# gate_a's matrix-vector product in a latent-flow layer: slabs taken in two runs of four and eight of one, each loaded one call ahead

## The chip, the cores and the metric

The kernel runs on one core of a Trainium2 chip. The core has a matrix engine (TensorE, PE in the profile, with PEld for its weight loads), a vector engine (VectorE, DVE), a scalar engine (ScalarE, ACT), GpSimd (POOL) and SyncE (SP), whose queue issues most of the loads from DRAM. On-chip memory is SBUF; TensorE writes to PSUM, which has eight banks here. The metric is the device time of one execution in microseconds (us), lower is better.

## The reference, cut to what matters

One layer of a flow-matching backbone with 128 context tokens and 256 latent tokens, width 2048, all in float32. A condition vector of each of the two groups is turned into six modulation vectors of width 2048:

```
mod = silu(cond) @ ada_w + ada_b          # ada_w: 2048 x (6 * 2048)
shift_a, scale_a, gate_a, shift_f, scale_f, gate_f = mod
h   = rmsnorm(x) * (1 + scale_a) + shift_a
q, k, v, o, gates, u = split(h @ w_in)
hm  = rmsnorm(bidirectional mLSTM(q, k, v, gates)) * sigmoid(o)
hp  = pooling mixer(u)
x   = x + gate_a * rmsnorm(concat(hm, hp) @ w_out)
h   = rmsnorm(x) * (1 + scale_f) + shift_f
x   = x + gate_f * rmsnorm(relu(h @ w1)**2 @ w2)
```

The change concerns how the second half of gate_a (columns 1024 to 2047 of it) is computed. It is not needed before the attention's output has gone through w_out.

## The kernel before, in words

All 384 tokens go through together. Activations stand transposed, as 16 k-tiles of 128 channels. Each float32 operand of a large product is split into a high and a low part (ScalarE copies the high part, L134; VectorE subtracts, L135), and three matmuls (`mm3`, L143 to L145) make one product.

The stages are: scale_a and shift_a with the projections u and v (to 203 us of the profile); the q and k gemms of head group 0, with pooling and gates beside them; three more q and k pairs, and then four o gemms, with attention beside them; the output projection `w_out`; then the MLP.

`gemm_T` walks through its weights in steps. One step loads one slab of weights of 512 KB by SP (`load_w`), splits it, and runs 4 k-tiles x 2 halves x 3 = 24 matmuls. A q or k gemm has 4 steps, so a pair has 8. At the end of a step the gemm calls its *feeds*: each feed is a Python generator with a rate, adds the rate to its due time at every step, and runs to its next `yield` once for every whole unit that is due. A feed thus sets between which gemm steps its instructions stand in the program.

The program is then ordered by a scheduler, in these stages for all engines: among instructions that it reckons to be ready, the one that stands first in the program goes first. It also gives out buffers: a load is put in an engine's queue when a buffer of its tag is free. So loads can run far ahead of their users, in the order of the program, and each engine's queue, SP's too, is then worked off in that fixed order.

Two feeds multiply the conditions by pieces of ada_w here, in two ways:

- `ada1` is gate_a's second half, by `ada_mat` (L215) on TensorE. It has 16 slabs of 512 KB: 4 parts of 256 columns by 4 groups of 4 of the 16 k-tiles. Each call loads one slab (L228) and issues its 4 matmuls (L232), each with 32 weight columns at one of four column groups of the array, so that the four run beside one another. A float32 matmul of this kind is recorded twice. The 64 matmuls add up in one PSUM bank. At the end ScalarE copies the bank (L238), four matmuls gather the rows (L241), and `ada_finish` adds the bias and multiplies by the norm's weights on VectorE (L249, L257). Its rate is 0.35.
- `ada2` is `mid_vec`, five times `ada_vec`: scale_f, shift_f and gate_a's first half, each in pieces of 1024 columns, by VectorE. A slab of 512 KB is loaded one ahead (L269), then two VectorE operations per slab (L280, L282) add it to an accumulator, of which there is one. After 16 slabs TensorE sums the accumulator over the partitions (`adav`, L293), and later `adaf` (L299) and `ada_finish` close it. Its rate is 1.5 from the second q and k pair on.

Slabs of both feeds have the tag `ada`, with four buffers (`N_ADA = 4`). Attention (L572 on) is a feed at rate 1 with its own VectorE, ScalarE and GpSimd work; its matmuls are `mb`, `s`, `k`, `sk`, `cu`, `num` and `inter`, and the feeds of a step are called with attention's first, then `ada1`, then `ada2`.

```
ada1 = Feed(ada_mat([(2, 8 + 2 * b, 2) for b in range(4)]), RATE_MAT)
...
qk(0, (fxt, fg_, fp_, ada1))
...
for g in range(1, 4):
    fa.append(Feed(attention(g - 1), 1.0))
    qk(g, (*fa[-2:], ada1, ada2))
```

Of the kernel before, what the change touches and what calls it, by code (L numbers as in the profile page):

```python
# [7 lines left out]
F32 = mybir.dt.float32  # L8
# [5 lines left out]
P = 128  # L14
D = 2048
# [13 lines left out]
N_ADA = 4  # L29
# [7 lines left out]
S_FIRST, S_LAST, N_LAST = 1, 6, 2  # L37
LAG = 4
RATES = (1.5, 1.3, 1.3)
RATE_MAT = 0.35  # L40


@with_exitstack
def hymba_kernel(
# [6 lines left out]
    nc = tc.nc  # L51
# [6 lines left out]
    adap = ada_scope.enter_context(tc.tile_pool(name="adap", bufs=1, side="right"))  # L58
# [6 lines left out]
    def bank(name):  # L65
        return psum.tile([P, 512], F32, tag="ps", name=name)
# [38 lines left out]
    cT = adap.tile([P, 16, 38], F32, name="cT")  # L105
# [106 lines left out]
    mod = const.tile([P, 6, KT, 2], F32, name="mod")  # L212
    aw = ada_w.rearrange("(p j) n -> p j n", j=16)

    def ada_mat(parts, tags=("ada",), raws=None):  # L215


        n, nk = len(parts), parts[0][2]
        w, nj = nk * P, 8 // nk
        ps = bank(f"ada_{parts[0][0]}_{parts[0][1]}")  # L220
        for b, (i, k0, _) in enumerate(parts):
            c0 = i * D + k0 * P
            for j0 in range(0, 16, nj):
                tag = tags[b % len(tags)]
                raw = raws.pop(0) if raws else None
                if raw is None:
                    raw = (wp if tag == "lo" else adap).tile([P, nj, w], F32, tag=tag, name=f"ada_raw_{i}_{k0}_{j0}", bufs=N_W if tag == "lo" else N_ADA)
                    nc.sync.dma_start(raw, aw[:, j0:j0 + nj, c0:c0 + w])  # L228
                for a in range(nj):
                    j = j0 + a  # L230
                    g = j % 4
                    nc.tensor.matmul(ps[32 * g:32 * g + 32, 0:w], cT[:, j, 6 - 2 * b:38 - 2 * b], raw[:, a, :],  # L232
                                     start=b == 0 and j < 4, stop=b == n - 1 and j >= 12)
                if b < n - 1 or j0 + nj < 16:
                    yield
        sb = adap.tile([P, 512], F32, tag="adasb", name=f"ada_sb_{parts[0][0]}_{parts[0][1]}", bufs=1)
        with tc.high_priority():
            nc.scalar.activation(sb[:, 0:w], ps[:, 0:w], AF.Copy)  # L238
        yield
        for k in range(nk):  # L240
            nc.tensor.matmul(ps[:, 256 + 8 * k:256 + 8 * k + 2 * n], sb[:, k * P:(k + 1) * P], cst[:, C_SEL, 0:2 * n], start=True, stop=True)  # L241
        for b, (i, k0, _) in enumerate(parts):
            ada_finish(i, k0, nk, ps[:, 256:256 + 8 * nk].rearrange("p (k r) -> p k r", r=8)[:, :, 2 * b:2 * b + 2])
        yield

    def ada_finish(i, k0, nk, ps):

        v = mod[:, i, k0:k0 + nk, :]
        nc.vector.tensor_tensor(  # L249
            v, ps,  # L250
            abias[:, i, k0:k0 + nk].unsqueeze(2).to_broadcast([P, nk, 2]), op=ALU.add)
        if i in (1, 4):
            w = nw[:, i // 2, k0:k0 + nk].unsqueeze(2).to_broadcast([P, nk, 2])
            nc.vector.scalar_tensor_tensor(v, v, 1.0, w, op0=ALU.add, op1=ALU.mult)
        elif i in (2, 5):
            w = nw[:, 1 if i == 2 else 3, k0:k0 + nk].unsqueeze(2).to_broadcast([P, nk, 2])
            nc.vector.tensor_tensor(v, v, w, op=ALU.mult)  # L257
# [50 lines left out]
    def first_ada():  # L308
        for k0, nk in ksteps:
            if k0 == 0:  # L310
                yield from ada_mat([(1, k0, nk)])
                yield from ada_mat([(0, k0, nk)], ("lo",))
            else:
                yield from ada_mat([(0, k0, nk), (1, k0, nk)])
# [66 lines left out]
    def load_chunk(s, ci, after=(), later=None):  # L381
        kind, c0, w = chunks[ci]
        ks = slice(ksteps[s][0], sum(ksteps[s]))
        if kind == "u":
            n, pieces = w, [(0, wv_in[:, ks, U0 + c0:U0 + c0 + w])]
        else:
            n, pieces = w * P, [(0, wv_in[:, ks, V0 + c0 * P:V0 + (c0 + w) * P])]
            if c0 == 6:
                pieces.append((n, wv_in[:, ks, 4 * M:4 * M + 32]))
                n += 32  # L390
        return load_w(pieces, f"{kind}_{c0}_{s}", ksteps[s][1] * n, after, later) + (n,)
# [8 lines left out]
    for s in range(NS):  # L400
        for ci, (kind, c0, w) in enumerate(chunks):
            k0, nk = ksteps[s]
            hi, lo, n = w_first if s == 0 and ci < 2 else load_chunk(s, ci, h_ins if s == 0 else ())
# [6 lines left out]
            for ps in [ways[n:n + 1] for n in range(3)] if s == ci == 0 else [ways]:  # L410
                for k in range(nk):
                    for i in range(3):
                        for a, b in ps:
                            nc.tensor.matmul(acc[i][:, 0:n], h[k0 + k][a][:, i * P:(i + 1) * P], (hi, lo)[b][:, k, :],  # L414
                                             start=k == 0 and a + b == 0, stop=k == nk - 1 and b == 1)
# [289 lines left out]
    def mid_vec():  # L705
        for i, q in ((4, 0), (4, 1), (3, 0), (3, 1), (2, 0)):
            yield from ada_vec(i, 1024 * q, 1024)

    ada1 = Feed(ada_mat([(2, 8 + 2 * b, 2) for b in range(4)]), RATE_MAT)
    ada2 = Feed(mid_vec(), RATES[0])  # L710

    def qk(g, feeds):
        gemm_T(w_in, [g * 256], hx, NTOK, evac_q, feeds, name="q")
        gemm_T(w_in, [M + g * 256], hx, NTOK, evac_k, feeds, name="k")
# [17 lines left out]
    vec.update(pool=adap, acc=accp, slab=1024, bufs=N_ADA)  # L732
    att = att_scope.enter_context(tc.tile_pool(name="att", bufs=2, reuse_waits="tile"))
    fa = []
    for g in range(1, 4):
        fa.append(Feed(attention(g - 1), 1.0))
        qk(g, (*fa[-2:], ada1, ada2))
# [23 lines left out]
    ps = bank("ps_nout")  # L761
# [43 lines left out]
    for cols in ([0, 256], [512], [768], [1024], [1280], [1536], [1792]):  # L805
        if cols[0] in (768, 1024, 1280):
            for m in range(2):
                n = len(early)
# [494 lines left out]
```

## Time and profile before

| | |
|---|---|
| median of 3 runs | 1694.27 us (1694.01 to 1696.2) |
| the profiled execution's own time | 1695.96 us |
| its span, first to last instruction | 1693.9 us |
| TensorE busy | 1663.3 us (98%) |
| VectorE busy | 1343.1 us (79%) |
| ScalarE busy | 752.6 us (44%) |
| granted TensorE clock, mean | 0.998 |

A row of a group has the line of the kernel, the engine, the operation, the tiles written and read, the shapes, and the count. In a timeline the first two columns are the start and the length in us; TensorE's matmuls overlap, so there the distance between starts tells more than the length. "x8" is eight like instructions in a row. "[0.40 <-DVE C L634]" is idle time before an instruction and what ended it. A row of waits reads: who waited, for whom, us in total, how many times, the longest.

### The profile page before, as it was taken

What the parts mean: (1) busy time and instruction counts of PE and PEld (TensorE: products, weight loads), DVE (VectorE), ACT (ScalarE), POOL (GpSimd) and SP (SyncE); (2) the same over time, 40 slices, a digit from 0 to 9 for tenths busy, and PEclk for the clock granted to TensorE, in tenths of its full rate; (3) what the DMA queues carried; (4) which work ended last, traced back from release to release, by engine and by line L of the source; (5) the groups of instructions that cost most, each with busy time, mean ns of one, the idle gap of its engine ahead of it and who ended that gap; (6) DMA issues with size and microseconds to landing.
All of it is one profiled execution on the core that took longest, in us unless ns stands there. A gap on an engine that the chain in (4) does not pass through costs nothing.

```text
span 1693.9 us, 28014 instructions
## 1 busy us (share of the span) xinstructions
PE 1663.3 (98%) x11025; PEld 1581.6 (93%) x11025; DVE 1343.1 (79%) x2000; ACT 752.6 (44%) x1225; POOL 155.5 (9%) x194
## 2 busy tenths in 40 slices
PE   6999999999999999999999999999999999999997
PEld 3887899999999989988999999999999999999996
DVE  3677759898999959997798588988588488588688
ACT  4432345555434336453444444444344444444443
POOL 0000002221002223540000000000000000000120
PEclk9999999999999999999999999999999999999999
DMA  9888957777788773754455345544344443433653
GB/s 309 294 291 288 305 160 253 229 250 247 241 278 286 262 246 112 218 157 136 152 181 186 98 137 163 167 150 137 112 142 126 132 137 111 152 121 108 189 184 134
DMA packets 262291, 320.95 MB, mean 189 GB/s; under 512 B 14752, under 2 KB 231440, under 8 KB 261776
## 3 DMA queue, kind: packets, MB, share of 16 engines
q1 hardware_dynamic: 254352, 303.41, 56.1%
q0 software_dynamic: 5856, 13.69, 2.8%
q10 hardware_dynamic: 1952, 2.07, 0.4%
q8 instruction: 86, 1.41, 0.3%
q14 instruction: 45, 0.37, 0.1%
HBM read 308.61 MB, written 10.51 MB: 188 GB/s over the span
## 4 chain that ended last, share of the span: by engine, by line
PE 82%; DVE 9%; DMA 5%; issue 3%; ACT 1%; POOL 0%; DVEq 0%; SPq 0%; ACTq 0%; POOLq 0%
PE acc_w L144 10%; PE acc_w L145 10%; PE acc_w L143 10%; DVE ada_acc L282 4%; PE y L1137 4%; PE y L1138 4%; PE y L1136 4%; PE v L414 3%; PE u L414 3%; PE y_yz L1136 2%; PE y_yz L1137 2%; PE y_yz L1138 2%; PE ada L232 2%; PE y L980 2%; PE y L978 2%
## 5 line engine op out<-in xcount | busy, mean ns | idle before, releaser
L144 PE MATMUL acc_w<-h2l,hi_w 128*128 128x384 f32 (+1 forms) x1024 | 345.9, 338 | 0.5 <-DVE h2l L930 0.5
L145 PE MATMUL acc_w<-h2h,lo_w 128*128 128x384 f32 (+1 forms) x1024 | 345.7, 338 | 0.0
L143 PE MATMUL acc_w<-h2h,hi_w 128*128 128x384 f32 (+1 forms) x1024 | 344.4, 338 | 1.2 <-ACT h2h L926 1.2
L135 DVE TENSOR_TENSOR lo_w<-raw_w,hi_w 128x1024 fp32r<-128x1024 f32 x152 | 185.6, 1223 | 136.1 <-ACT hi_w L134 135.0
L282 DVE SCALAR_TENSOR_TENSOR ada_acc<-ada_raw,sg,ada_acc 128x1024 f32<-128x1024 f32 (+1 forms) x240 | 259.5, 1113 | 2.8 <-DMA ada_raw<-in_ada_w_dram 2.7
L134 ACT ACTIVATE hi_w<-raw_w 128x1024 fp32r<-128x1024 f32 x152 | 161.0, 1059 | 212.4 <-PE acc_w L144 91.3
L143 PEld LDWEIGHTS acc_w<-h2h,hi_w 128*128 128x128 f32 x1024 | 192.2, 188 | 2.8 <-ACT h2h L926 2.0
L144 PEld LDWEIGHTS acc_w<-h2l,hi_w 128*128 128x128 f32 x1024 | 192.4, 188 | 1.3 <-DVE h2l L930 0.8
L145 PEld LDWEIGHTS acc_w<-h2h,lo_w 128*128 128x128 f32 x1024 | 192.4, 188 | 0.5 <-DVE lo_w L135 0.4
L1122 ACT ACTIVATE hi_t<-w 128x1024 fp32r<-128x1024 f32 x104 | 109.7, 1061 | 117.9 <-DVE w L1158 33.2
L1123 DVE TENSOR_TENSOR lo_t<-w,hi_t 128x1024 fp32r<-128x1024 f32 x104 | 126.6, 1223 | 15.2 <-ACT hi_t L1122 14.9
L1123 DVE TENSOR_TENSOR lo_b<-w,hi_b 128x1024 fp32r<-128x1024 f32 x78 | 95.4, 1223 | 39.8 <-ACT hi_b L1122 39.6
L1122 ACT ACTIVATE hi_b<-w 128x1024 fp32r<-128x1024 f32 x78 | 82.7, 1061 | 97.8 <-PE acc_w L144 65.0
L134 ACT ACTIVATE hi_wo<-raw_wo 128x1024 fp32r<-128x1024 f32 x32 | 34.1, 1064 | 80.4 <-DMA raw_wo<-in_w_out_dram 43.8
L856 ACT ACTIVATE z<-acc_w 128x384 f32<-128x384 f32 x54 | 26.3, 487 | 75.1 <-PE acc_w L145 75.1
L892 POOL DMA_DIRECT2D gf_dram<-gfT x1 | 0.5, 521 | 551.8 <-DVE gfT L891 551.8
L135 DVE TENSOR_TENSOR lo_wo<-raw_wo,hi_wo 128x1024 fp32r<-128x1024 f32 x32 | 41.3, 1295 | 9.5 <-ACT hi_wo L134 9.5
L414 PE MATMUL v<-hi_v,hh 128*128 128x384 f32 (+1 forms) x144 | 47.9, 332 | 0.0
L414 PE MATMUL v<-hi_v,hl 128*128 128x384 f32 (+1 forms) x144 | 46.5, 323 | 0.0
L414 PE MATMUL v<-lo_v,hh 128*128 128x384 f32 (+1 forms) x144 | 46.5, 323 | 0.0
L232 PE MATMUL ada<-ada_raw,cT 128*32 128x256 f32 x656 | 45.0, 395 | 1.1 <-DMA ada_raw<-in_ada_w_dram 1.1
L143 PE MATMUL acc_k<-hh,hi_k 128*128 128x384 f32 x128 | 44.5, 348 | 0.0
(2250 smaller groups left out, 4578.0 us busy)
## 6 DMA issues: line engine op xcount, KB each, us to landing
ada_raw<-in_ada_w_dram SPq DMA_DIRECT2D x170, 512.0 KB, 4.7
raw_w<-in_w_dram SPq DMA_DIRECT2D x152, 512.0 KB, 4.1
w<-in_w_dram SPq DMA_DIRECT2D x104, 512.0 KB, 4.1
raw_wo<-in_w_out_dram SPq DMA_DIRECT2D x32, 512.0 KB, 5.0
raw_u<-in_w_in_dram SPq DMA_DIRECT2D x16, 512.0 KB, 8.6
raw_q<-in_w_in_dram SPq DMA_DIRECT2D x16, 512.0 KB, 4.7
raw_k<-in_w_in_dram SPq DMA_DIRECT2D x16, 512.0 KB, 4.6
raw_o<-in_w_in_dram SPq DMA_DIRECT2D x16, 512.0 KB, 5.3
```

The source lines that it names most:

```text
L134: nc.scalar.activation(hi[:, 0:n], raw[:, 0:n], AF.Copy)
L135: low = lambda: nc.vector.tensor_tensor(lo[:, 0:n], raw[:, 0:n], hi[:, 0:n].bitcast(F32), op=ALU.subtract)
L143: nc.tensor.matmul(ps, lh, rh, start=start, stop=False)
L144: nc.tensor.matmul(ps, lh, rl, start=False, stop=False)
L145: mm3.ins = nc.tensor.matmul(ps, ll, rh, start=False, stop=stop).ins
L282: nc.vector.scalar_tensor_tensor(acc[:, g, :], raw[:, a, :], cj, acc[:, g, :], op0=ALU.mult, op1=ALU.add)
L414: nc.tensor.matmul(acc[i][:, 0:n], h[k0 + k][a][:, i * P:(i + 1) * P], (hi, lo)[b][:, k, :], start=k == 0 and a + b == 0, stop=k == nk - 1 ...
L1122: nc.scalar.activation(hi, raw, AF.Copy)
L1123: nc.vector.tensor_tensor(lo, raw, hi.bitcast(F32), op=ALU.subtract)
L1136: nc.tensor.matmul(acc, xh, wh, start=start and j == 0, stop=False)
L1137: nc.tensor.matmul(acc, xh, wl, start=False, stop=False)
L1138: nc.tensor.matmul(acc, xl, wh, start=False, stop=stop and j == 3)
```

## The change: what it does

`ada1` gets a generator of its own, `ada_gate`. It has the same 16 slabs in the same order, the same 64 matmuls and one bank, but its list of runs, (4, 4, 1, 1, 1, 1, 1, 1, 1, 1), says how many slabs one call multiplies. The first call only loads the slabs of the first run. Each further call issues the matmuls of one run and then asks for the slabs of the next run. After the last run it goes on, without a `yield` between, to the closing work, which is cut out of `ada_mat` as `ada_rows` and is otherwise unchanged.

The rate is 0.375 during the first q and k pair (8 steps, so 3.0 calls) and 0.25 from the second pair on (one call every 4 steps). Before it was 0.35 throughout.

```diff
-RATE_MAT = 0.35
+RATE_MAT = 0.375, 0.25
...
+    def ada_gate(parts, runs):
+        n = len(parts)
+        ps = bank("ada_gate")
+        todo, ready = [(b, i, k0, j0) for b, (i, k0, _) in enumerate(parts) for j0 in range(0, 16, 4)], []
+        def load(m):
+            for b, i, k0, j0 in todo[:m]:
+                raw = adap.tile([P, 4, 256], F32, tag="ada", name=f"ada_raw_{i}_{k0}_{j0}", bufs=N_ADA)
+                nc.sync.dma_start(raw, aw[:, j0:j0 + 4, i * D + k0 * P:i * D + k0 * P + 256])
+                ready.append((b, j0, raw))
+            del todo[:m]
+        load(runs[0])
+        yield
+        for m, ahead in zip(runs, runs[1:] + (0,)):
+            for b, j0, raw in ready[:m]:
+                for a in range(4):
+                    j = j0 + a
+                    g = j % 4
+                    nc.tensor.matmul(ps[32 * g:32 * g + 32, 0:256], cT[:, j, 6 - 2 * b:38 - 2 * b], raw[:, a, :],
+                                     start=b == 0 and j < 4, stop=b == n - 1 and j >= 12)
+            del ready[:m]
+            load(ahead)
+            if ahead:
+                yield
+        yield from ada_rows(parts, ps)
...
+        yield from ada_rows(parts, ps)
+
+    def ada_rows(parts, ps):
+        n, nk = len(parts), parts[0][2]
+        w = nk * P
         sb = adap.tile([P, 512], F32, tag="adasb", name=f"ada_sb_{parts[0][0]}_{parts[0][1]}", bufs=1)
...
-    ada1 = Feed(ada_mat([(2, 8 + 2 * b, 2) for b in range(4)]), RATE_MAT)
+    ada1 = Feed(ada_gate([(2, 8 + 2 * b, 2) for b in range(4)], (4, 4) + 8 * (1,)), RATE_MAT[0])
...
     fa = []
+    ada1.rate = RATE_MAT[1]
     for g in range(1, 4):
```

## The prediction

> **What bounds the kernel now.** I read the page first, then the list of what TensorE waited for, then the busy time by stretch. The page's first part says that TensorE is busy almost throughout; a busy TensorE alone proves little, so I looked for its waits in the stretch in which gate_a's slabs run, from the first q gemm (203 us) to the middle of the output projection (560 us).
>
> ```profile
> PE 1663.3 (98%) x11025; PEld 1581.6 (93%) x11025; DVE 1343.1 (79%) x2000; ACT 752.6 (44%) x1225; POOL 155.5 (9%) x194
> ```
> ```profile
> PE acc_wo L145 <- DVE lo_wo L135: 1.1, 2, 0.8
> PE inter L651 <- DVE hs L661: 0.8, 1, 0.8
> PE inter L651 <- DVE C L634: 0.4, 1, 0.4
> ```
>
> Those three rows are all that TensorE waited for in 357 us: 2.3 us. So TensorE's own work sets the time here, and a wait that disappears can give back 2.3 us at most. All three end with VectorE, which is the nearest second (columns: length, then busy of PE, PEld, DVE, ACT, POOL, granted clock, DMA share, GB/s):
>
> ```profile
> 224.00:244.00 20.00, 20.00 (x127) 18.97 (x126) 8.14 (x18) 9.33 (x16) 0.00 (x0) 1.00 0.40 125
> 264.00:284.00 20.00, 20.00 (x138) 19.47 (x137) 18.78 (x30) 7.88 (x19) 3.96 (x4) 1.00 0.81 264
> 284.00:304.00 20.00, 20.00 (x130) 19.34 (x129) 18.50 (x36) 11.24 (x35) 5.46 (x5) 1.00 0.70 230
> 304.00:324.00 20.00, 20.00 (x135) 19.05 (x134) 15.84 (x23) 12.06 (x31) 5.02 (x5) 1.00 0.83 258
> 344.00:364.00 20.00, 20.00 (x125) 19.25 (x126) 19.41 (x25) 11.96 (x33) 5.26 (x3) 1.00 0.78 245
> 364.00:384.00 20.00, 18.78 (x126) 17.87 (x126) 19.49 (x34) 8.43 (x24) 3.66 (x5) 1.00 0.83 268
> 520.00:542.00 22.00, 20.95 (x118) 20.48 (x118) 22.00 (x19) 6.98 (x10) 3.80 (x2) 1.00 0.85 266
> ```
>
> The reader sees where the 2.3 us arise: in 364 to 384, where VectorE is busy 19.49 of 20 us, and in 520 to 542, where it never rests. The clock is full throughout, so it plays no part. In 224 to 244, VectorE and the DMA engines are half idle: that is where the change moves work to.
>
> **The change, part by part.** *Matmuls.* The number of slabs (16), of matmuls (64, each recorded as two) and of bytes stays. What changes is how many slabs stand together. A slab alone, and a run of four slabs (32 records) from the first phase, between the same three-product matmuls:
>
> ```profile
> 242.58 0.34 PE L145 MATMUL poolo<-p21h,lo_pw 128*128 128x384 f32 x1
> 242.85 0.64 PE L232 MATMUL ada<-ada_raw,cT 128*32 128x256 f32 x8
> 243.42 0.45 PE L143 MATMUL acc_k<-hh,hi_k 128*128 128x384 f32 x1
> 243.70 0.34 PE L144 MATMUL acc_k<-hl,hi_k 128*128 128x384 f32 x1
> 243.88 0.33 PE L145 MATMUL acc_k<-hh,lo_k 128*128 128x384 f32 x1
> ```
> ```profile
> 177.31 0.34 PE L414 MATMUL v<-lo_v,hh 128*128 128x384 f32 x1
> 177.58 1.93 PE L232 MATMUL ada<-ada_raw,cT 128*32 128x256 f32 x32
> 179.45 0.44 PE L414 MATMUL v<-hi_v,hh 128*128 128x384 f32 x1
> 179.73 0.34 PE L414 MATMUL v<-hi_v,hl 128*128 128x384 f32 x1
> ```
>
> The lone slab takes 243.70 - 242.58 = 1.12 us between its neighbours' starts; undisturbed neighbours start 0.175 us apart (243.70 to 243.88), two such steps are 0.35, so it costs 0.77. The run takes 179.73 - 177.31 - 0.35 = 2.07 us, where four lone slabs take 3.08: each run saves 1.01 us, because entering and leaving the small matmuls is paid once. Sixteen lone slabs cost 12.3 us; two runs and eight lone ones 4.14 + 6.16 = 10.3. That is **-2.0 us**. No matmul of gate_a is among the waits listed above; all of them in one row, the first and last start behind the durations:
>
> ```profile
> L232 PE MATMUL ada<-ada_raw,cT x128: 379/390/405, 222.6 to 470.3; 128*32 128x256 f32 x128
> ```
>
> Bounds: nothing, if the runs end where VectorE sets the pace, and -2.2 with reading error. I take -2.0.
>
> *Steps.* Before, due time grows 0.35 a step (a step is four k-tiles of one weight slab): slabs at steps 3, 6, 9, 12 and so on to 46 (222.6 to 470.3 above). After, 0.375 over eight steps gives calls at steps 3, 6 and 8: loads only, then a run, then a run; 0.25 gives a lone slab every fourth step, 12 to 40, and the closing four matmuls at step 44, still in the o gemms. Step 8 of the q/k pair thus begins the attention 2 x 2.07 - 2 x 0.77 = 2.6 us later than before; by step 20 three lone slabs stand where four did, so 1.8 us; the sum is only reached at the end of the o gemms.
>
> *DMAs.* The slabs of gate_a and those of VectorE's matvec (scale_f, shift_f) share four buffers and SP's queue. SP's issues before (L228 gate_a or the first phase, L269 VectorE's):
>
> ```profile
> 178.28 0.37 SPq L228 DMA_DIRECT2D ada_raw<-in_ada_w_dram  x1
> 182.76 0.41 SPq L228 DMA_DIRECT2D ada_raw<-in_ada_w_dram  x1
> 186.07 0.43 SPq L228 DMA_DIRECT2D ada_raw<-in_ada_w_dram  x1
> 186.61 0.44 SPq L269 DMA_DIRECT2D ada_raw<-in_ada_w_dram  x1
> 243.55 0.40 SPq L269 DMA_DIRECT2D ada_raw<-in_ada_w_dram  x1
> 245.12 0.37 SPq L128 DMA_DIRECT2D raw_q<-in_w_in_dram  x1
> 254.89 0.37 SPq L228 DMA_DIRECT2D ada_raw<-in_ada_w_dram  x1
> ```
>
> Loads go out as soon as a buffer is free, in the order of the program: three slabs of gate_a and one of scale_f fill the buffers by 187 us, and the fourth gate_a slab, used at step 12, is asked for at 254.89, over 20 us ahead. So "a step ahead" buys nothing: no lone slab was late. In the new order the four first buffers all hold gate_a; the same bytes move at the same time, at no cost. Slabs 5 to 8 can be asked for only as step 6's run frees buffers: 242.85 less step 3's 0.77 is 242.1, and at 0.43 a slab (1.87 / 4) they go out from 242.6 to about 244.4. How fast four in a row land:
>
> ```profile
> L228 SPq DMA_DIRECT2D ada_raw<-in_ada_w_dram x4: 367/457/458, 168.9 to 170.5; - x4
> DMA to landing us min/median/max: 3.5/5.8/8.0
> ```
>
> So the last is there by 252.4. Step 8's run starts at 255.38 - 1.54 + 2.07 = 255.9:
>
> ```profile
> 255.38 0.34 PE L143 MATMUL acc_q<-hh,hi_q 128*128 128x384 f32 x1
> ```
>
> A margin of 3.5 us: **0**, and 0 to +2 as bounds (a landing half as slow again). Behind these four on SP stand weights such as raw_q at 245.12, the fourth of its gemm: used three steps of 24 x 0.175 = 4.2 us after 255.38, past 268. Four issues of 0.46 us don't reach that cover of over 20 us; GpSimd's queue gets nothing new.
>
> *VectorE's first slab.* This is what the change makes late. Scale_f's first slab was there by 187 us; now its four buffers are gate_a's until step 8's run, slab 9 takes the first that comes free, and scale_f's first goes out near 257. With the quickest landing of the burst, 3.5 us, VectorE begins at about 260.5 rather than 251.06:
>
> ```profile
> 251.06 1.42 DVE L280 TENSOR_SCALAR ada_acc<-ada_raw,sg 128x1024 f32<-128x1024 f32 x2
> 252.38 2.48 DVE L282 SCALAR_TENSOR_TENSOR ada_acc<-ada_raw,sg,ada_acc 128x1024 f32<-128x1024 f32 x2
> 255.91 2.48 DVE L282 SCALAR_TENSOR_TENSOR ada_acc<-ada_raw,sg,ada_acc 128x1024 f32<-128x1024 f32 x2
> 259.43 2.49 DVE L282 SCALAR_TENSOR_TENSOR ada_acc<-ada_raw,sg,ada_acc 128x1024 f32<-128x1024 f32 x2
> ```
> ```profile
> 312.62 1.27 DVE L282 SCALAR_TENSOR_TENSOR ada_acc<-ada_raw,sg,ada_acc 128x1024 f32<-128x1024 f32 x1
> ```
> ```profile
> 324.26 1.06 PE L293 MATMUL adav<-ada_acc,cst 128*32 128x512 f32 x8
> ```
>
> Deferred are these four rows, 1.42 + 2.48 + 2.48 + 2.49 = 8.9 us. The sums were ready at 313.9 and TensorE took them at 324.26, a cover of 10.4 us, which the 1.8 us of later steps stretch to 12.2. VectorE's rest in the three windows from 264 to 324 is 1.2 + 1.5 + 4.2 = 6.9 us, with the 1.8 it is 8.7: what was deferred just about fits. I take **0**; the next matvec starts only after 324 anyway and is not touched. If the cover fails, VectorE is full for 60 us; of two windows as full beside attention, 344 to 364 cost nothing and 364 to 384 1.2 us of waits, so the bound is 3 x 1.2 = +3.6.
>
> *The end of gate_a.* Its copy, four matmuls and eight small VectorE operations move from the start of the output projection into the o gemms: same work, 8 x about 0.15 = 1.2 us of VectorE moved out of the stretch where lo_wo was late by 1.1. And step 28's slab will stand before the two late inter waits (1.2 us), giving VectorE 0.77 us more there. Gains from 0 to 2.3; I take 0, since every shifted VectorE order brings its own waits. The PSUM bank is held from step 6 to 44 instead of 3 to 49: no wait showed on it, 0.
>
> **The sum.** The profiled execution took 1695.96 us, 2.1 more than its span of 1693.9; minus 2.0 it would be 1694.0. That execution lies near the slowest of the runs shown (1696.2); on their median the sum is 1694.27 - 2.0 = **1692.3 us**.
>
> **The rivals.** *Faster, the waits go too.* -2.0 - 2.3 = -4.3: 1690.0. For it: the two moves just named work at exactly those waits. Against: VectorE stays as full in both places.
>
> *Slower, VectorE does not catch up.* If scale_f's start at 260.5 is not made good by 326, attention's own VectorE operations queue behind deferred slabs (+3.6), and the first matvec's end slides; the accumulator is one, so the next matvecs slide with it, through windows in which VectorE rests 0.6 and 0.5 us (344 to 384), into the output projection, where all 22.00 of 22 us are taken. Between none and all of the 8.9 us gets there; I price half: -2.0 + 3.6 + 4.4 = +6.0, 1700.3. It decides when VectorE is more than about 2 us late at the first adav. For it: a fit of 8.9 in 8.7 is no margin. Against: 344 to 384 was as full and cost 1.2 us in all.
>
> One row makes this rival's fit tighter. A GpSimd select stretched a VectorE operation from 1.28 to 1.66 us:
>
> ```profile
> 265.67 1.78 POOL L601 TENSOR_SCALAR_AFFINE_SELECT e<-e 128x768 f32<-128x768 f32 x1 [2.50 <-DVE ws L597]
> ```
> ```profile
> L282 DVE SCALAR_TENSOR_TENSOR ada_acc<-ada_raw,sg,ada_acc x30: 1262/1280/1664, 252.4 to 312.6; 128x1024 f32<-128x1024 f32 x30
> ```
>
> [...] The trace shows 0.38 for one, which is what the rest of this text goes by.
>
> *It doesn't reach the end.* VectorE's pace, not TensorE's, might set when the output projection ends (the 20.95 of 22 busy us above); then the 2.0 us turn into waits: 1694.3.
>
> **How the numbers follow.** This measurement can tell about 0.2% (3.4 us) from no change. As forecast, 0.45 (same); not reaching the end, 0.13 (same); waits gone too, 0.22: faster; VectorE late, 0.20: slower. That leaves 0.58 for same. The range begins at 1689.3 (1690.0 less 0.7 for scatter between runs) and ends at 1699.0, short of the slower rival's own price, since part of that rival stops earlier. The likeliest case alone spans 1691.1 (half of the 2.3 us of waits gone) to 1694.3 (the second run's slabs 2 us late).
>
> **What would show it.** Two groups of 32 gate_a records near 242 and 256 us, each about 1.87 us, and eight groups of 8 every fourth step; no wait of ada matmuls on their DMA at the second run (if there is one of over 1 us, the landing estimate is wrong); the first ada_acc at 260 or 261; the first adav near 326 with no TensorE wait before it (a wait there, or waits of inter and num on VectorE over 3 us in 260 to 330, make the slower rival true); lo_wo's 1.1 us still there or gone; the h2 stage beginning some 2 us earlier. If the time falls by more than 4.5 us or rises at all beyond 3.4, something outside this sum did it.

## The result, and the profile after

The change makes the kernel slower: 1705.78 us in the median (1704.11 to 1711.9) against 1695.24 (1694.01 to 1697.4) of the kernel before on the same chip, six runs each, a ratio of 1.0058 with a 95% interval of 1.0045 to 1.007. That is 10.5 us, past the upper end of the stated range (1699.0). The profiled execution took 1706.46 us over a span of 1704.6, at a mean granted clock of 0.998 as before (over all six executions of the change it was 0.9962; more on that below).

The page's first part of the kernel after shows TensorE with hardly more to do than before (1664.6 us for 1663.3), in a span that is 10.7 us longer:

```profile
PE 1664.6 (98%) x11025; PEld 1582.3 (93%) x11025; DVE 1342.5 (79%) x2000; ACT 750.0 (44%) x1225; POOL 179.9 (11%) x194
```

Where the time goes is read from one stretch: from the first q matmul to the first matmul of w1. Busy time by stretch, kernel before (columns as in the prediction):

```profile
202.90:629.00 426.10, 423.11 (x2697) 402.72 (x2696) 360.92 (x526) 191.74 (x422) 74.47 (x69) 1.00 0.76 248
```

The same stretch of the kernel after:

```profile
204.80:638.00 433.20, 423.56 (x2699) 403.72 (x2697) 360.74 (x526) 190.01 (x422) 99.09 (x69) 1.00 0.75 244
```

It is 7.1 us longer. VectorE does the same work (360.9 and 360.7 us), and TensorE's time without work grows from 3.0 us (426.10 - 423.11) to 9.6 (433.20 - 423.56). The other 3.6 us of the 10.7 lie outside: 1.9 before the first q matmul (202.9 to 204.8) and 1.7 behind w1's start (1693.9 - 629.0 = 1064.9, and 1704.6 - 638.0 = 1066.6). Up to the first q matmul the two programs have the same instructions in the same order on every engine (one load of SyncE has another source, gate_a's fourth slab instead of scale_f's first), so those 1.9 us are scatter between executions: two kernels of the experiments that are identical to the change up to that point reached it at 201.9 and 206.4. The last part scatters too, from 1063.9 to 1067.0 over the kernels profiled here.

What TensorE waits for from 200 to 640 us in the kernel after, most costly first; of before the prediction showed 2.3 us, all told it was 3.0:

```profile
PE acc_q L145 <- DVE lo_q L135: 3.8, 3, 2.7
PE inter L684 <- DVE hs L694: 2.0, 2, 1.2
PE num L677 <- DVE e L647: 1.8, 1, 1.8
...
PE acc_wo L145 <- DVE lo_wo L135: 0.5, 1, 0.5
...
PE inter L684 <- DVE C L667: 0.3, 1, 0.3
```

The largest is new and is no wait of the attention: the q gemm waits for the low part of its weights. Followed backwards, it leads to the buffers of the slabs. SyncE's queue after (L224 gate_a, L302 VectorE's slabs, L128 weights):

```profile
244.76 3.01 SPq L224 DMA_DIRECT2D ada_raw<-in_ada_w_dram  x4
258.69 0.39 SPq L224 DMA_DIRECT2D ada_raw<-in_ada_w_dram  x1
259.17 8.58 SPq L302 DMA_DIRECT2D ada_raw<-in_ada_w_dram  x4
296.73 0.38 SPq L128 DMA_DIRECT2D raw_q<-in_w_in_dram  x1
```

Slabs 5 to 8 of gate_a take all four buffers at 244.76. They come free with the second run at 257.99. Slab 9 takes the first, and scale_f's first slab is asked for at 259.17. The tile of the slabs, from 258 to 268 us, and its times from request to landing:

```profile
L302 SPq DMA_DIRECT2D ada_raw<-in_ada_w_dram x4: 328/437/597, 259.2 to 267.4; - x4
DMA to landing us min/median/max: 3.6/6.0/8.2
```

The view has three landings: 6.0 us for gate_a's slab 9, asked for at 258.69, 8.2 for scale_f's third slab, asked for at 260.2, and 3.6 for its fourth, asked for by itself at 267.4. VectorE's timeline, with the first slab, an operation of attention and two of the weights' low parts behind it:

```profile
265.98 1.42 DVE L313 TENSOR_SCALAR ada_acc<-ada_raw,sg 128x1024 f32<-128x1024 f32 x2 [5.74 <-DMA ada_raw<-in_ada_w_dram]
...
289.39 0.35 DVE L694 SCALAR_TENSOR_TENSOR hs<-num,dn,hs 128x128 f32<-128x128 f32 x1
...
295.44 1.22 DVE L135 TENSOR_TENSOR lo_k<-raw_k,hi_k 128x1024 fp32r<-128x1024 f32 x1
...
308.40 1.22 DVE L135 TENSOR_TENSOR lo_q<-raw_q,hi_q 128x1024 fp32r<-128x1024 f32 x1
```

VectorE stands still for 5.74 us and begins at 265.98, where it began at 251.06 before. Its order is fixed once the program is built, so what stands behind that slab moves with it. The same split of the k weights, behind the same 16 operations on slabs, comes at 277.35 before and at 295.44 here. From before:

```profile
277.35 1.22 DVE L135 TENSOR_TENSOR lo_k<-raw_k,hi_k 128x1024 fp32r<-128x1024 f32 x1
...
283.42 0.35 DVE L661 SCALAR_TENSOR_TENSOR hs<-num,dn,hs 128x128 f32<-128x128 f32 x1
```

Counted from the first q matmul the split is 16.2 us late, more than the first slab (13.0, below), because the order itself is another one: the scheduler has put the first hs and other operations of attention ahead of this split, behind which they stood before. How much of the loss comes from the wait while the kernel runs and how much from the new order, no run here separates; both come with the late slab. Only then is its raw buffer free, so the next raw_q is asked for at 296.73 (before, at 278.64), and it lands too late for ScalarE's high part and so for the low part at 308.40. ScalarE's and TensorE's timelines after:

```profile
306.46 1.06 ACT L134 ACTIVATE hi_q<-raw_q 128x1024 fp32r<-128x1024 f32 x1 [2.58 <-DMA raw_q<-in_w_in_dram]
```
```profile
309.68 0.61 PE L145 MATMUL acc_q<-hh,lo_q 128*128 128x384 f32 x2 [2.69 <-DVE lo_q L135]
```

The windows of the kernel after show that VectorE is never full behind the late slab:

```profile
264.00:284.00 20.00, 20.00 (x135) 19.47 (x134) 18.02 (x23) 11.44 (x30) 5.09 (x4) 1.00 0.75 249
284.00:304.00 20.00, 18.76 (x116) 18.07 (x116) 17.42 (x37) 7.93 (x27) 3.84 (x4) 1.00 0.66 216
304.00:324.00 20.00, 16.66 (x104) 15.20 (x103) 18.14 (x27) 10.61 (x30) 5.34 (x3) 1.00 0.71 231
```

From 264 to 324 it still rests 2.0 + 2.6 + 1.9 = 6.4 us, though it is in arrears; before, without arrears, it rested 6.9. Late in the stretch, from 304 to 324, TensorE (16.66 of 20 us), the DMA engines (0.71) and VectorE (18.14) all idle a little and wait for one another in a fixed order: TensorE 3.3 us for VectorE's lo_q, ScalarE 2.6 in front of it for the load of raw_q.

### The profile page after: what moved, and what is told of

It reads as the page before. It is cut to its first block, busy times and chain, and to the rows that moved or that the text cites. A ratio compares the mean times of both kernels' runs of the same rounds, so it can differ in the third digit from the quotient of the medians.

```text
span 1704.6 us, 28008 instructions
## 1 busy us (share of the span) xinstructions
PE 1664.6 (98%) x11025; PEld 1582.3 (93%) x11025; DVE 1342.5 (79%) x2000; ACT 750.0 (44%) x1225; POOL 179.9 (11%) x194
## 3 DMA queue, kind: packets, MB, share of 16 engines
q10 hardware_dynamic: 1952, 2.07, 0.4%
## 4 chain that ended last, share of the span: by engine, by line
PE 69%; DVE 14%; DMA 8%; issue 5%; ACT 2%; POOL 1%; SPq 0%; DVEq 0%; ACTq 0%; POOLq 0%
PE acc_w L143 9%; PE acc_w L144 9%; PE acc_w L145 9%; DVE ada_acc L315 5%; PE y L1171 4%; PE y L1170 4%; PE y L1172 4%; PE u L447 3%; PE v L447 3%; PE y_yz L1171 2%; PE y_yz L1170 2%; PE y_yz L1172 2%; DMA ada_raw<-in_ada_w_dram 2%; PE y L1012 2%; PE y L1013 2%
## 5 line engine op out<-in xcount | busy, mean ns | idle before, releaser
L144 PEld LDWEIGHTS acc_w<-h2l,hi_w 128*128 128x128 f32 x1024 | 192.6, 188 | 1.3 <-DVE h2l L964 0.8
L823 POOL TENSOR_TENSOR sqa<-sqa,sq_mo 128x384 f32<-128x384 f32 x13 | 48.0, 3696 | 70.7 <-ACT sq_mo L822 70.0
L447 PE MATMUL v<-hi_v,hh 128*128 128x384 f32 (+1 forms) x144 | 47.8, 332 | 0.0
L145 PE MATMUL acc_q<-hh,lo_q 128*128 128x384 f32 x128 | 43.3, 340 | 3.8 <-DVE lo_q L135 3.8
```

What stands on the lines that cost most here:

```text
L144: nc.tensor.matmul(ps, lh, rl, start=False, stop=False)
L145: mm3.ins = nc.tensor.matmul(ps, ll, rh, start=False, stop=stop).ins
```

## The experiments

The first theory, A in the expectations, was: the late start of scale_f's first slab costs the time, because it makes everything behind it on VectorE late. Against it stood that the runs themselves, or the asking a call ahead, cost it. The expectations name these by letters (B is the runs, C the asking ahead), and the kernels by labels (x1, x3 and so on), which stand here in brackets.

**The first load a pair earlier (x1).** The first four slabs are asked for before the first q and k pair, so the runs come at steps 3 and 6, and the buffers are free for scale_f sooner. The runs of four stay.

```diff
+    next(ada1.gen)
     fxt = Feed(store_xT(), 3.0)
```

> The changed kernel with one thing moved: the first call of the feed, which only loads four slabs, is made before the first q and k pair instead of at step 3. The runs of four then stand at steps 3 and 6 instead of 6 and 8, and the third call, the first lone slab, at step 8; nothing else is edited. Theory A (VectorE's first slab came late because gate_a held all four buffers until step 8): the buffers come free at step 6, about 244 us, VectorE's first ada_acc starts within 3 us of the 251 us of before instead of at 266, the waits for lo_q (3.8 us) and for e (1.8 us) go, and the time is 1691 to 1696 us. Theory B (the runs themselves harm: 1.9 us blocks on TensorE and bursts of four loads beside the weights): as many runs and bursts as in the changed kernel, so 1702 to 1708 us.

1698.22 us in the median of ten runs, against 1696.95 of the kernel before: ratio 1.0005 (0.9995 to 1.0015). By the median the loss is gone, but no gain has come in its place. VectorE's first slab in this kernel:

```profile
254.60 1.41 DVE L313 TENSOR_SCALAR ada_acc<-ada_raw,sg 128x1024 f32<-128x1024 f32 x2
```

It stands at 50.8 us behind the first q matmul (203.8), where before had 48.2 and the change 61.2. No wait for lo_q is left. The profiled execution was the slowest of the ten (1702.25): from the first q matmul to w1 it took 431.2 us, 5.1 more than before, with waits of 2.1 us for hs, 1.9 for lo_o and 1.9 for lo_wo. So the profile shows where VectorE starts, not how the median execution came to lose nothing.

**The same, with the buffers held back (x8).** To change the start alone, three of the four buffers are filled with an idle tile at the end of the first pair; it is released behind the copy of a k tile. Runs, calls and slabs stay as in the kernel just shown. A memset of one column and three one-column copies are added.

```diff
+    held = [adap.tile([P, 4, 256], F32, tag="ada", name=f"held{n}", bufs=N_ADA) for n in range(3)]
+    for t in held:
+        nc.gpsimd.memset(t[:, 0, 0:1], 0.0)
+    with tc.issue_after(evac_k.ins):
+        for n, t in enumerate(held):
+            nc.scalar.activation(hcol[:, n:n + 1], t[:, 0, 0:1], AF.Copy)
```

> The kernel of x1 with three of the four buffers of the tag ada taken at the end of the first pair by tiles that hold one zero column each, and let go by a copy of that column on ScalarE behind the copies of k, at about 257 us. No matmul, load or VectorE operation is added. This makes VectorE's first slab late and nothing else. Theory A: VectorE starts at 262 to 268 us, and the time is 8 to 12 us above x1, about that of the changed kernel, 1702 to 1708 us. Theory B: the runs stand as in x1, so the time is within 2 us of x1.

1706.24 us, ratio 1.006 (1.0044 to 1.0077, four runs): the whole loss is back. Its first slab on VectorE:

```profile
265.51 2.03 DVE L313 TENSOR_SCALAR ada_acc<-ada_raw,sg 128x1024 f32<-128x1024 f32 x2
```

What its TensorE waited for from 200 to 640 us:

```profile
PE inter L684 <- DVE hs L694: 4.1, 2, 3.7
PE hT L733 <- DVE hs L697: 2.5, 1, 2.5
PE acc_o L145 <- DVE lo_o L135: 1.6, 1, 1.6
...
```

The first slab starts 62.7 us behind the first q matmul (202.8). About the same lateness thus costs the same time within the intervals, though TensorE stalls at other operations than in the change. One of these stalls also shows in the granted clock (PE busy, clock, DMA share, GB/s):

```profile
388.00:392.00 4.00, 2.23 (x8) 0.68 0.42 131
```

That window holds the end of the 3.7 us for hs. The runs of four without the late start lose nothing, and with it they lose all that the change loses: the late start is the cause, not the runs as such.

**Other shapes of the runs.** One run of four and twelve lone slabs (x4); two runs of two (x5); and no run at all, but each slab asked for a call ahead (x3).

```diff
-    ada1 = Feed(ada_gate([(2, 8 + 2 * b, 2) for b in range(4)], (4, 4) + 8 * (1,)), RATE_MAT[0])
+    ada1 = Feed(ada_gate([(2, 8 + 2 * b, 2) for b in range(4)], (4,) + 12 * (1,)), RATE_MAT[0])
```
```diff
-    ada1 = Feed(ada_gate([(2, 8 + 2 * b, 2) for b in range(4)], (4, 4) + 8 * (1,)), RATE_MAT[0])
+    ada1 = Feed(ada_gate([(2, 8 + 2 * b, 2) for b in range(4)], (2, 2) + 12 * (1,)), RATE_MAT[0])
```
```diff
-RATE_MAT = 0.375, 0.25
+RATE_MAT = 0.35, 0.35
...
-    ada1 = Feed(ada_gate([(2, 8 + 2 * b, 2) for b in range(4)], (4, 4) + 8 * (1,)), RATE_MAT[0])
+    ada1 = Feed(ada_gate([(2, 8 + 2 * b, 2) for b in range(4)], 16 * (1,)), RATE_MAT[0])
```

> The changed kernel with runs of (4,) and then twelve lone slabs, at the same rates: one run of four at step 6, one lone slab at step 8, the end of gate_a in the output projection. Theory A: at step 6 three buffers come free for VectorE, so its first slab is asked for near 245 us and VectorE starts near 251; one run saves 1.0 us: 1692 to 1697 us. Theory B: one run does half of the harm of two: about 1700 us.

> The changed kernel with runs of (2, 2) and then twelve lone slabs, at the same rates. Gate_a asks for two slabs at a time, but the second two go into the two free buffers at once, so that VectorE's first slab goes out when step 6 frees two buffers (244 us) and its second only at step 8. Theory A (the start of VectorE's matvec decides): VectorE starts at 250 to 255 us, with one slab in hand, and the time is 1 to 5 us above before, between x1 and the changed kernel. Were it only the number of slabs in a run, two runs of two would cost about half of what the changed kernel lost, 4 to 6 us.

> The changed kernel's feed with sixteen lone slabs and the rate of before, 0.35 throughout: only the loading a call ahead is left of the change. Theory A: gate_a holds one buffer more than before for three steps at a time, VectorE's first slab is still there by 190 us, so 1694 to 1698 us. A third theory, C, that loading a call ahead alone takes the buffers that VectorE's matvec needs through the whole attention: 1699 us or more.

One run: 1699.06 us, ratio 1.0018 (1.0008 to 1.0029). Runs of two: 1700.03, 1.0014 (1.0004 to 1.0023). Lone ahead: 1700.57, 1.0022 (1.0011 to 1.0032). Ten runs each. In all three VectorE started on time, 48.9, 47.8 and 47.4 us behind the first q matmul (before 48.2), and 2 to 4 us were still lost. So A does not explain them: its ranges had 1692 to 1697 us for the first and 1694 to 1698 for the third. The second lies in its range of 1 to 5 us above before, but without the late start that A gave as the reason. C's time for the third (1699 or more) came true; its reason, too few buffers for VectorE, isn't seen. The loss falls from 10 us to about 3, and that rest isn't the late start. The profile of the third was its quickest execution (1697.2) and shows no place for it. That of the second (1698.23) is 3.2 us longer than before from the first q matmul to w1 (429.3), with 2.9 us of waits for hs, before 0.8. The granted clock, on the mean of all runs, doesn't show the rest either (0.9971 to 0.9973 for these three kernels, 0.9975 to 0.9976 for the runs of before beside them: 0.0005 of 1700 is 0.9 us at most, an estimate from these clocks). The cause of the rest stays open.

**One run, asked for early (x10).** Both mends together: the early first load, one run of four, and a rate that spreads the lone slabs.

```diff
-RATE_MAT = 0.375, 0.25
+RATE_MAT = 0.375, 0.3
...
-    ada1 = Feed(ada_gate([(2, 8 + 2 * b, 2) for b in range(4)], (4, 4) + 8 * (1,)), RATE_MAT[0])
+    ada1 = Feed(ada_gate([(2, 8 + 2 * b, 2) for b in range(4)], (4,) + 12 * (1,)), RATE_MAT[0])
...
+    next(ada1.gen)
```

> As x1, the first load made before the first pair, but with one run of four, at step 3, and twelve lone slabs after it, the rate of the attention at 0.3. Theory A: gate_a's next slabs and VectorE's first go out at 223 us already, VectorE starts by 252 us as before, and the one run saves up to 1.0 us: from 2 us below to 2 us above before. It is slower than that only if a slab more of gate_a in the buffers, as in x3, is what cost x3 its 3.6 us.

1697.99 us, ratio 1.0005 (0.9994 to 1.0015): the same as before, once more without the gain.

**What TensorE's time is worth here (x9, x11).** The gain of 2.0 us was counted in full in the prediction. Two kernels made from the one before measure that by larger amounts. One shortens the matmuls of gate_a's second half, but for the first slab, to 8 of 256 columns, so most of that half is left out. The other issues each of them twice, so that this half is doubled.

```diff
+    u = 8 if parts[0][0] == 2 and (b, j0) != (0, 0) else w
-    nc.tensor.matmul(ps[32 * g:32 * g + 32, 0:w], cT[:, j, 6 - 2 * b:38 - 2 * b], raw[:, a, :],
+    nc.tensor.matmul(ps[32 * g:32 * g + 32, 0:u], cT[:, j, 6 - 2 * b:38 - 2 * b], raw[:, a, 0:u],
```
```diff
+    for m in range(2 if parts[0][0] == 2 else 1):
         nc.tensor.matmul(ps[32 * g:32 * g + 32, 0:w], cT[:, j, 6 - 2 * b:38 - 2 * b], raw[:, a, :], ...
```

> The kernel before, with the matmuls of gate_a's second to sixteenth slab cut to 8 of their 256 columns; loads, slabs, steps and the places of the matmuls stay. Most of gate_a's second half is thereby left out of the result. A lone slab keeps the cost of entering and leaving and loses about its 0.43 us of streaming, so that TensorE has 15 x 0.35 to 0.43 = 5 to 6 us less to do. Theory D (TensorE's own work sets the time in this stretch, as the prediction's sum had it): 4 to 6 us faster than before. Theory E (what TensorE saves there comes back as waits for VectorE): within 2 us of before.

> The kernel before, with each of gate_a's second-half matmuls of the sixteen slabs issued twice in a row, so that this half of gate_a comes out doubled; everything else stays. TensorE has 16 x 0.43 = 6.9 us more to do. Theory D: 5 to 8 us slower than before. Theory E: VectorE gets the same time more to catch up, and the time rises by less than 4 us.

TensorE's timeline of the shortened kernel around a lone slab:

```profile
242.17 0.34 PE L145 MATMUL poolo<-p21h,lo_pw 128*128 128x384 f32 x1
242.44 0.25 PE L233 MATMUL ada<-ada_raw,cT 128*32 128x8 f32 x8
...
242.90 0.34 PE L144 MATMUL acc_k<-hl,hi_k 128*128 128x384 f32 x1
```

Even so short a slab costs 242.90 - 242.17 - 0.35 = 0.38 us, half of the 0.77 of a whole one: that is what changing over to the small matmuls and back takes. Fifteen slabs save 15 x 0.39 = 5.8 us. Measured: 1694.1 against 1697.3, ratio 0.9984 (0.9971 to 0.9997), or 2.7 us, between the ranges of D (4 to 6) and E (within 2). From the first q matmul to w1 in that kernel (length, then TensorE's busy time):

```profile
202.40:626.40 424.00, 418.40 (x2699) 1.00 0.78 249
```

TensorE has 4.7 us less work than before (423.11 - 418.40), but its idle time rises from 3.0 to 5.6, and the stretch shortens by only 2.1. The doubled kernel in the same view:

```profile
204.20:637.70 433.50, 430.16 (x2827) 1.00 0.76 244
```

Here the work grows by 7.0 us, the idle time stays at 3.3, and the stretch is 7.4 longer, in the slowest of its seven executions (1706.72). Over all seven the median was 1703.97 against 1697.3, ratio 1.003 (1.0018 to 1.0041), or 5.1 us, at the lower end of D's range (5 to 8). In these two profiles added work counts in full and saved work by about half, as idle time takes the rest. Over all runs the intervals are too wide to show such a difference: 0.5 to 4.9 us came of the 5.8 saved, and 3.1 to 7.0 of the 7.0 added. What they show is that part of the saved work reaches the end.

**VectorE's feed slower (x12, x13).** If the deferred slabs are what crowds out the weights, the change must lose less when scale_f and shift_f are called less often in the attention pairs and more often in the o gemms.

```diff
-RATES = (1.5, 1.3, 1.3)
+RATES = (1.35, 1.5, 1.3)
```

> The changed kernel with VectorE's matvec fed at 1.35 instead of 1.5 calls a step beside the attention and at 1.5 instead of 1.3 beside the o gemms (32.4 + 24 calls instead of 36 + 20.8, about the same sum). The first adav then stands at step 14 instead of 12 of its feed, some 10 us later, which gives back most of the cover that the late first slab took; gate_a's runs and buffers stay. Theory A, in the form that the loss is VectorE's backlog against the place of its work in the program: half or more of the 10 us goes, 1697 to 1702 us. If the late start costs by itself wherever the matvec's end stands: 1704 us or more.

> The same two rates in x1, where VectorE starts in time. If VectorE's fullness beside the attention is what turned the 2.0 us that x1's runs save on TensorE into waits, they come through: 1694 to 1696 us with a before of 1697. If the o gemms and the output projection pay for it instead, lo_o and lo_wo are late and the time is 1698 us or more.

The change with these rates: 1702.9 us against 1696.42, ratio 1.0037 (1.0023 to 1.005, ten runs), just above the range that A gave (1697 to 1702). The early-load kernel with them: 1702.68, ratio 1.0043 (1.0028 to 1.0059, four runs). First and last start of the gemms' matmuls in the kernel before:

```profile
L143 PE MATMUL acc_q<-hh,hi_q x128: 331/338/446, 202.9 to 368.7; 128*128 128x384 f32 x128
L143 PE MATMUL acc_o<-hh,hi_o x128: 333/338/443, 395.5 to 478.6; 128*128 128x384 f32 x128
```

In the change:

```profile
L143 PE MATMUL acc_q<-hh,hi_q x128: 331/337/441, 204.8 to 377.2; 128*128 128x384 f32 x128
L143 PE MATMUL acc_o<-hh,hi_o x128: 333/338/440, 405.9 to 488.2; 128*128 128x384 f32 x128
```

In the change with the slower feed:

```profile
L143 PE MATMUL acc_q<-hh,hi_q x128: 331/337/443, 201.9 to 372.1; 128*128 128x384 f32 x128
L143 PE MATMUL acc_o<-hh,hi_o x128: 331/337/522, 397.4 to 484.7; 128*128 128x384 f32 x128
```

From the first q to the first o matmul the kernel before takes 192.6 us, the change 201.1 and the slower feed 195.5: two thirds of the 8.5 us come back where the deferred slabs stood. But its o gemms, from the first to the last start, take 87.3 us instead of 82.3 (before, 83.1). What its TensorE waited for from 200 to 640 us:

```profile
PE acc_o L145 <- DVE lo_o L135: 3.2, 1, 3.2
PE acc_wo L145 <- DVE lo_wo L135: 1.8, 2, 1.0
...
```

The wait on the weights' low part has moved from q to o, 3.2 us in one piece, ending at 466.75. It has an echo, which the windows around it show (TensorE's busy time, then the granted clock, the DMA share and GB/s):

```profile
464.00:468.00 4.00, 1.25 (x4) 0.63 0.44 150
468.00:472.00 4.00, 4.00 (x15) 0.51 0.75 231
472.00:476.00 4.00, 4.00 (x24) 1.00 0.79 256
```

From 468 to 472, behind the stall, the clock is 0.51, and TensorE does 15 matmuls in 4 us rather than 24: by estimate 9 x 0.175 = 1.6 us more, beside the 3.2 of the wait itself; together that is 4.8 of the 5.0 us that the o gemms take longer. The early-load kernel, which had no loss to mend, only pays: it lost 0.4% to the same rates, with a longest wait for lo_o of 3.1 us and a mean granted clock of 0.9955 over its four runs. So where the slabs go, a split of weights is late, and in the change with the slower feed a clock of 0.51 in the 4 us behind the stall adds to it.

## Why the prediction was wrong, point by point

**Right: the runs' own cost and their timing.** TensorE's timeline after, around the two runs and at the first adav:

```profile
243.79 0.34 PE L145 MATMUL poolo<-p21h,lo_pw 128*128 128x384 f32 x1
244.06 1.93 PE L235 MATMUL ada_gate<-ada_raw,cT 128*32 128x256 f32 x32
...
246.20 0.34 PE L144 MATMUL acc_k<-hl,hi_k 128*128 128x384 f32 x1
...
257.99 1.94 PE L235 MATMUL ada_gate<-ada_raw,cT 128*32 128x256 f32 x32
...
334.37 1.04 PE L326 MATMUL adav<-ada_acc,cst 128*32 128x512 f32 x8
```

A run costs 246.20 - 243.79 - 0.35 = 2.06 us (forecast 2.07), the two stand at 244 and 258, and the second doesn't wait for its slabs. Step 2 (DMAs, 0) holds for gate_a's own slabs.

**The step that failed: "VectorE's first slab", taken at 0.** Three of its numbers were wrong, in one direction. First, the start. The forecast was 260.5; it came at 265.98. Of the 5.5 us, 1.9 are the scatter of the first phase, 3.3 are the landing (requested at 259.17 and in use at 265.98, 6.8 us, where the quickest landing of a burst, 3.5, was taken, though this slab stands in a burst too, behind gate_a's slab 9), and 0.3 the request. Second, VectorE's start, counted from the first q matmul, was late by 61.2 - 48.2 = 13.0 us rather than by 9.4 (260.5 - 251.06), of which 8.9 were work. Third, and this matters most, the rests of VectorE were added up as room for it (8.7 us). None of it was made good, as the last slab of the first matvec shows:

```profile
328.53 1.28 DVE L315 SCALAR_TENSOR_TENSOR ada_acc<-ada_raw,sg,ada_acc 128x1024 f32<-128x1024 f32 x1
```

It ends at 329.81, 125.0 us behind the first q matmul, where before it ended at 313.89, 111.0 behind it: 14.0 us late, after a start that was 13.0 late. In the measured windows from 264 to 324 VectorE still rested 6.4 us. Those rests are waits of its fixed order for an operand (2.0 us for the first slab, 1.0 for a later one, 2.0 for GpSimd, 0.7 for ScalarE, 0.7 for a store), and work that stands behind in the same order can't be moved into them.

The cover that the step relied on, the 10.4 us in front of adav, did hold: TensorE took the sums at 334.37, 4.6 us after they were ready, without a wait. It was the wrong thing to look at, since the splits of the weights stand between the slabs and have less cover. The first adav did come 8.2 us later (334.37 - 204.8 less 324.26 - 202.9), but because TensorE was late: it had stood still for 5.0 us by then (124.46 us busy of 129.50, before 121.30 of 121.30), and 3.2 us more of work stood in front of adav. So of the signs named for the slower case one came, over 2 us late at the first adav, though not for the reason given, and the others didn't: no wait at adav, and 1.2 us of waits of inter and num from 260 to 330, where over 3 were named.

**"The next matvec is not touched" fell with it:** with adav at 334.37 and one accumulator, the next piece began late too (its first slab at 339.03, before at 328.62).

**The rival "VectorE does not catch up" had the late engine right, its path only in part, and too small a price.** It gave +6.0. It priced attention's own VectorE operations behind the slabs, by windows that had cost 1.2 us each; inter and num waited 2.0 + 1.8 + 0.3 = 4.1 us, before 1.2, a rise of 2.9 (the bound was 3.6). What it left out is the weights' splits, which stand in the same order: lo_q cost another 3.8, and they in turn delay the request of the next weights through the raw buffers. It left out the clock too: over all executions it was lower by 0.9975 - 0.9962 = 0.0013 than in the 26 runs of before that stand beside the shortened and the doubled kernel, by estimate some 2.2 us of 1700. Most of that is the one execution of 1711.9 us, with a clock of 0.992; the other five have 0.997 on the mean, and the profiled one shows none of it, so the median owes little to the clock. The second term (+4.4, the slide into the output projection) is not what was seen: from the first o matmul to w1's first the change took 638.0 - 405.9 = 232.1 us and before 629.0 - 395.5 = 233.5.

**"Matmuls", -2.0, is right for the runs themselves and doesn't show in the time.** TensorE's busy time in the stretch didn't fall by 2.0 but rose by 0.45. A matmul of 384 columns is recorded 0.34 us long while undisturbed neighbours start 0.175 us apart, so a stall of up to 0.16 us between two is counted as busy there. The tile acc_q alone, from 203 to 634 us (TensorE's busy time first behind the length), before and after:

```profile
203.00:634.00 431.00, 70.59 (x384) 66.62 (x383) 3.82 (x8) 1.00 0.76 248
```
```profile
203.00:634.00 431.00, 71.68 (x384) 66.61 (x384) 3.80 (x8) 1.00 0.76 246
```

These are 1.1 us for the same 384 matmuls; the rest isn't assigned. In the kernels without the late start the 2.0 us, or 1.0 with one run, didn't show in the time either (1.0005 both). Two readings fit this: the saved time turned into waits, as about half of it did in the shortened kernel, or it came through and paid for the asking ahead, which these kernels do as well and which alone cost 0.2%. So whether the rival "it doesn't reach the end" was true is not shown.

**"The end of gate_a", 0,** can't be told apart from the rest. The wait for lo_wo went from 1.1 to 0.5 us. Where VectorE and GpSimd work at the same time the rows show two things. The longest operation on a slab beside the selects took 1.88 us in the change and 1.66 before, where one alone takes 1.28: 0.60 us more, where the prediction went by 0.38. And in the output projection, where VectorE is busy 58.6 of 60 us (500 to 560), it is GpSimd's operations that take longer: its 13 additions take 48.0 us instead of 22.3, one of them alone 26.3. Before, VectorE's took longer there (a pair of slab operations beside the additions took 4.02 us instead of 2.47). What makes operations of the two engines longer beside one another, no run here shows. It isn't the loss: the kernel with one run asked for early has the long additions too (47.8 us) and lost nothing. From the page of the change and of that kernel:

```profile
L823 POOL TENSOR_TENSOR sqa<-sqa,sq_mo 128x384 f32<-128x384 f32 x13 | 48.0, 3696 | 70.7 <-ACT sq_mo L822 70.0
```
```profile
L824 POOL TENSOR_TENSOR sqa<-sqa,sq_mo 128x384 f32<-128x384 f32 x13 | 47.8, 3681 | 70.9 <-ACT sq_mo L823 70.3
```

**Open.** Why asking a call ahead alone costs 0.2%, and a single run started on time about as much. Giving gate_a buffers of its own, which would take the cause away instead of moving it, wasn't tried, so it isn't shown that it helps. No version that does the whole computation was faster than the kernel before.

## What to carry to other kernels

Loads that are asked for in runs out of buffers shared with another user take these buffers from that user, so ask who is next in line and cost its start with the landing time of a burst (here 6.0 to 8.2 us), not with the quickest one (3.5). In a fixed order a late operand holds up all that stands behind it, splits of weights and so their loads included, and the idle time of an engine is not room to catch up in (here the last slab was 14.0 us late after a start 13.0 late, past 6.4 us of rests). Cover has to be counted at every operation behind the late one, and not only at the last. Where a second engine is nearly as full, time taken from the busiest need not come through whole (here 2.7 of 5.8 us did in the median).

## What was not expected of the hardware

In the slower-feed kernel the granted clock was 0.63 in the window of 4 us in which a stall of TensorE of 3.2 us ended, 0.51 in the next and 1.00 in the one after (above), and around the end of a stall of 3.7 us in the kernel with held buffers it was 0.68. In the early-load kernel, the 4 us behind a wait for hs of 2.1 us show 0.65:

```profile
384.00:388.00 4.00, 4.00 (x18) 0.65 0.94 269
```

The change's own longest stall, 2.7 us, left the clock at 1.00 in its profile (in each window of 4 us from 300 to 316). So length alone doesn't decide here: 2.1 us went with a lower clock and 2.7 us didn't. What does decide, no run here shows. The prediction said that the clock plays no part; it held in the two profiles compared, but not in every kernel here.

Of four requests of 512 KB between 258.69 and 260.2 us, the first landed after 6.0 us and the last after 8.2; the next, with none in the 7 us before it, took 3.6. The same instructions, up to the first q matmul, took between 201.9 and 206.4 us in three executions, as much as many an edit of this kernel is worth; two profiles have to be compared from a common point behind that phase. And changing over to the small column-group matmuls and back costs 0.38 us even where they have hardly any work (8 of 256 columns), half the price of a lone slab.
